# Cosine similarity of rows: loading the last block in thirteen shrinking pieces of x and y in turn, chaining its sums, and storing its results as a column

## The chip, the cores and the metric

The kernel runs on one core of one Trainium2 chip. The time of a run is the time of one execution on the device, in microseconds (us). The profile is one further execution, and its span (first to last instruction) is about 2 us shorter than the time: 1254.4 us of 1256.4 us for the kernel before. Runs of one kernel agree within about 0.8 us here (b_col, one of the experiments: 1.3 us).

Names of engines: DVE is VectorE, ACT is ScalarE, PE is TensorE, SP is SyncE, which issues the DMA transfers. "SPq" in a line is SP's sequencer.

## The reference, cut to what matters

Two float32 inputs, 8192 rows of 8192 columns each; one float32 result per row.

```python
def reference(x, y):                       # 8192 x 8192 each
    x_norm = np.linalg.norm(x, axis=1, keepdims=True)
    y_norm = np.linalg.norm(y, axis=1, keepdims=True)
    return np.sum(x * y, axis=1) / (x_norm.squeeze() * y_norm.squeeze() + 1e-8)
```

Each element is read once: 537 MB in all. The work on a row is three sums: x·y, x·x and y·y.

## The kernel before

The rows form 64 blocks of 128. A block is a tile of x and a tile of y, 128 partitions by 8192 columns, 4 MB each, with two buffers per input. For every block but the last, each tile is loaded by one transfer; DVE sums x·y over the whole tile, and ACT squares and sums x, then y:

```python
nc.vector.tensor_tensor_reduce(out=prod_s, in0=xt, in1=yt, scale=1.0, scalar=0.0,
    op0=mult, op1=add, accum_out=xy_acc[:, t:t + 1])
nc.scalar.activation(out=sq_s, in_=xt, func=Square, accum_out=xx_acc[:, t:t + 1])
nc.scalar.activation(out=sq_s, in_=yt, func=Square, accum_out=yy_acc[:, t:t + 1])
```

The last block (number 63) is loaded as x in two halves, then y in pieces of 2048, 2048, 2048, 1024 and 1024 columns. Its end is what this document is about:

```python
# [cut: DVE squares the first 2048 columns of x, ACT the other 6144]
for k, (a, b) in enumerate(YCH):           # five pieces of y
    nc.scalar.activation(out=sq_s[:, a:b], in_=yt[:, a:b], func=Square, accum_out=yyp[:, k:k + 1])
    nc.vector.tensor_tensor_reduce(out=prod_s[:, a:b], in0=xt[:, a:b], in1=yt[:, a:b],
        scale=1.0, scalar=0.0, op0=mult, op1=add, accum_out=xyp[:, k:k + 1])
# [cut: fold the partial sums; nn = xx*yy; den = sqrt(nn); rcp = 1/den; res = xy*rcp, two columns]
nc.tensor.transpose(out=res_t_ps_last[0:2, :], in_=res[:, tcols], identity=ident)
nc.vector.tensor_copy(out=res_row_last[0:2, :], in_=res_t_ps_last[0:2, :])
nc.sync.dma_start(out=out_v[last - 1:last + 1, :], in_=res_row_last[0:2, :])
```

A result column has one value in each of the 128 partitions. The transpose turns it into a row, so the store writes 512 bytes in one piece for each block.

Of the kernel before, what the change touches and what calls it, by code (L numbers as in the profile page):

```python
# [7 lines left out]


@with_exitstack  # L10
def kernel(
# [6 lines left out]
    nc = tc.nc  # L18
    P = nc.NUM_PARTITIONS

    n_rows, n_cols = x.shape
    assert n_rows % P == 0
    n_tiles = n_rows // P

    fp32 = mybir.dt.float32
    bf16 = mybir.dt.bfloat16

    xv = x.rearrange("(t p) k -> t p k", p=P)
    yv = y.rearrange("(t p) k -> t p k", p=P)

    xpool = ctx.enter_context(tc.tile_pool(name="xpool", bufs=2))
    ypool = ctx.enter_context(tc.tile_pool(name="ypool", bufs=2))
    sqpool = ctx.enter_context(tc.tile_pool(name="sqpool", bufs=1))
    prodpool = ctx.enter_context(tc.tile_pool(name="prodpool", bufs=1))
    accpool = ctx.enter_context(tc.tile_pool(name="accpool", bufs=1))
    finpool = ctx.enter_context(tc.tile_pool(name="finpool", bufs=1))
    psumpool = ctx.enter_context(tc.tile_pool(name="psum", bufs=1, space=bass.MemoryType.PSUM))

    xtiles = [
        xpool.tile([P, n_cols], fp32, tag="x", name=f"xt{t}")  # L40
        for t in range(n_tiles)
    ]
    ytiles = [
        ypool.tile([P, n_cols], fp32, tag="y", name=f"yt{t}")
        for t in range(n_tiles)
    ]

    last = n_tiles - 1

    HALF = n_cols // 2  # L50

    XCH = [(0, HALF), (HALF, n_cols)]
    Q = n_cols // 8
    YCH = [(0, 2 * Q), (2 * Q, 4 * Q), (4 * Q, 6 * Q), (6 * Q, 7 * Q), (7 * Q, n_cols)]

    def issue_dma(t):
        if t == last:
            for a, b in XCH:
                nc.sync.dma_start(out=xtiles[t][:, a:b], in_=xv[t, :, a:b])  # L59
            for a, b in YCH:  # L60
                nc.sync.dma_start(out=ytiles[t][:, a:b], in_=yv[t, :, a:b])  # L61
        else:
            nc.sync.dma_start(out=xtiles[t], in_=xv[t])  # L63
            nc.sync.dma_start(out=ytiles[t], in_=yv[t])  # L64

    issue_dma(0)
    issue_dma(1)

    dummy = finpool.tile([P, 1], fp32, tag="dummy")
    nc.scalar.memzero(dummy)  # L70
    nc.scalar.sqrt(out=dummy, in_=dummy)  # L71

    ident = finpool.tile([P, P], fp32, tag="ident")
    make_identity(nc, ident)

    xx_acc = accpool.tile([P, n_tiles], fp32, tag="xx")
    yy_acc = accpool.tile([P, n_tiles], fp32, tag="yy")
    xy_acc = accpool.tile([P, n_tiles], fp32, tag="xy")

    prod_s = prodpool.tile([P, n_cols], bf16, tag="prod")  # L80
    sq_s = sqpool.tile([P, n_cols], bf16, tag="sq")

    res = finpool.tile([P, n_tiles], fp32, tag="res")
    nn = finpool.tile([P, n_tiles], fp32, tag="nn")
    den = finpool.tile([P, n_tiles], fp32, tag="den")
    rcp = finpool.tile([P, n_tiles], fp32, tag="rcp")
    res_t_ps = psumpool.tile([n_tiles, P], fp32, tag="res_t_ps")
    res_t = finpool.tile([n_tiles, P], fp32, tag="res_t")
    res_t_ps_last = psumpool.tile([2, P], fp32, tag="res_t_ps_last")
    res_row_last = finpool.tile([2, P], fp32, tag="res_row_last")  # L90
    out_v = out.rearrange("(t p) -> t p", p=P)

    def compute_tile(t):
        xt = xtiles[t]
        yt = ytiles[t]
        nc.vector.tensor_tensor_reduce(  # L96
            out=prod_s,
            in0=xt,
            in1=yt,
            scale=1.0,  # L100
            scalar=0.0,
            op0=mybir.AluOpType.mult,
            op1=mybir.AluOpType.add,
            accum_out=xy_acc[:, t:t + 1],
        )
        nc.scalar.activation(  # L106
            out=sq_s,
            in_=xt,
# [28 lines left out]
    for t in range(n_tiles - 1):  # L137
        if t + 2 < n_tiles:
            issue_dma(t + 2)
# [114 lines left out]
```

## Time and profile before

| | |
|---|---|
| time | 1256.36 us (1256.19 to 1256.38, 3 runs) |
| span of the profiled run | 1254.4 us |
| period of a block | 19.4 us (e.g. y of block 61 lands at 1209.5, of block 62 at 1228.9) |
| DVE and ACT work in a block | 8.69 us; 2 x 7.03 + 2 x 0.19 = 14.4 us |
| last load packet, last multiply, end | 1248.9, 1251.66, 1254.4 us |

Lines of the page of the kernel before. In the group lines: line, engine, operation, tiles, shapes, count; then busy us and mean ns of one; then idle time just before them and what ended it.

```profile
span 1254.4 us, 933 instructions
...
q1 hardware_dynamic: 19220, 536.91, 99.5%
...
DMA 76%; DVE 22%; SPq 1%; issue 1%; DVEq 0%; PE 0%; ACT 0%
...
L96 DVE CUSTOM_DVE_ANT_0 prod_s<-xt,yt 128x8192 bf16<-128x8192 f32 x63 | 547.6, 8692 | 687.5 <-DMA yt<-in_y_dram 687.5
...
L112 ACT ACTIVATE sq_s<-yt 128x8192 bf16<-128x8192 f32 x63 | 443.0, 7031 | 164.2 <-DMA yt<-in_y_dram 164.2
...
L186 DVE CUSTOM_DVE_ANT_0 prod_s<-xt,yt 128x2048 bf16<-128x2048 f32 (+1 forms) x5 | 9.2, 1864 | 1.6 <-DMA yt<-in_y_dram 1.5
```

The load queue is busy 99.5% of the time, and DVE sits idle for 687.5 us before its whole-block products, until a load of y lands. So the loads bound the kernel, and only what comes after the last loads, the tail, can be shortened.

The view by stretches of the kernel before, with busy time of each engine, then the granted clock, the DMA share and GB/s:

```profile
...
core 0: us, PE busy (x) PEld busy (x) DVE busy (x) ACT busy (x) POOL busy (x), PEclk, DMA share, GB/s
...
1236.00:1246.00 10.00, 0.00 (x0) 0.00 (x0) 8.59 (x8) 9.38 (x10) 0.00 (x0) 1.00 1.00 413
1246.00:1249.00 3.00, 0.00 (x0) 0.00 (x0) 2.82 (x3) 3.00 (x5) 0.00 (x0) 1.00 0.18 70
1249.00:1252.45 3.45, 0.37 (x1) 0.08 (x1) 2.60 (x9) 1.85 (x7) 0.00 (x0) 1.00 0.00 0
1252.45:1254.40 1.95, 0.00 (x0) 0.00 (x0) 0.00 (x0) 0.00 (x0) 0.00 (x0) 1.00 0.00 1
```

From 1246 us on, most DMA engines have finished and a few lagging ones carry on (share 0.18). In the last 1.95 us no compute engine works: that is the store. The timeline of the same kernel (start us, length us, engine, line, operation) shows the steps between:

```profile
...
1236.10 1.91 ACT L167 ACTIVATE sq_s<-xt 128x2048 bf16<-128x2048 f32 x1
...
1248.17 1.04 ACT L180 ACTIVATE sq_s<-yt 128x1024 bf16<-128x1024 f32 x1
...
1249.21 1.04 ACT L180 ACTIVATE sq_s<-yt 128x1024 bf16<-128x1024 f32 x1
...
1249.55 1.22 DVE L186 CUSTOM_DVE_ANT_0 prod_s<-xt,yt 128x1024 bf16<-128x1024 f32 x1
...
1250.38 0.21 ACT L200 ACTIVATE yy_fold_s<-yyp 128x5 f32<-128x5 f32 x1
...
1250.81 0.16 DVE L204 TENSOR_REDUCE xy_acc<-xyp 128x1 f32<-128x5 f32 x1
...
1251.07 0.20 ACT L212 ACTIVATE den<-nn 128x2 f32<-128x2 f32 x1 [0.39 <-DVE nn L208]
...
1251.50 0.16 DVE L217 TENSOR_TENSOR res<-xy_acc,rcp 128x2 f32<-128x2 f32 x1
...
1251.72 0.37 PE L221 MATMUL res_t_ps_last<-ident,res 128*2 128x128 f32 x1 [31.64 <-DVE res L217]
1252.13 0.28 DVE L222 COPY res_row_last<-res_t_ps_last 2x128 f32<-2x128 f32 x1 [0.46 <-PE res_t_ps_last L221]
1252.43 0.27 SPq L223 DMA_DIRECT2D out_dram<-res_row_last  x1
```

The last product ends at 1249.55 + 1.22 = 1250.77, the last multiply at 1251.50 + 0.16 = 1251.66; the transpose and the copy take until 1252.41; from the issue of the store (1252.43) to the end of the span are 1.97 us. A backlog is work that is ready but has to queue for its engine.

### The profile page before, as it was taken

Reading aid. Unit: us, or ns where it says so; the run is one execution under the profiler, and the core shown is the slowest. Engines: PE = TensorE matmul, PEld = TensorE weight load, DVE = VectorE, ACT = ScalarE, POOL = GpSimd, SP = SyncE. Lnnn points to the kernel's source line nnn. Section 1 sums busy time; section 2 is a strip of 40 time slices with the busy share of each in tenths; the row PEclk is TensorE's granted clock in tenths of the full one; section 3 lists DMA queues with packets and bytes.
Section 4 is the critical chain, followed back from the end, with each engine's and each line's share of the span. In section 5 each row is a group of like instructions: output and inputs, shape, how many; then the busy total and the mean of one; then the engine's idle time right before and its main releaser. Section 6 shows DMA issues by size and latency. Waiting matters only on the chain.

```text
span 1254.4 us, 933 instructions
## 1 busy us (share of the span) xinstructions
PE 0.8 (0%) x2; PEld 0.2 (0%) x2; DVE 561.6 (45%) x147; ACT 915.0 (73%) x276; POOL 0.7 (0%) x6
## 2 busy tenths in 40 slices
PE   0000000000000000000000000000000000000000
PEld 0000000000000000000000000000000000000000
DVE  2354353443534535445354353453544525445356
ACT  5777767776777767776777767776777767776777
POOL 0000000000000000000000000000000000000000
DMA  9999999999999999999999999999999999999997
GB/s 401 435 435 435 429 430 428 435 434 435 429 429 430 434 433 435 429 428 432 434 434 435 428 428 432 435 434 434 428 428 433 435 433 433 427 430 432 435 434 307
DMA packets 19227, 536.97 MB, mean 428 GB/s; under 512 B 2132, under 2 KB 2196, under 8 KB 2452
## 3 DMA queue, kind: packets, MB, share of 16 engines
q1 hardware_dynamic: 19220, 536.91, 99.5%
q14 instruction: 7, 0.06, 0.0%
HBM read 536.87 MB, written 0.03 MB: 428 GB/s over the span
## 4 chain that ended last, share of the span: by engine, by line
DMA 76%; DVE 22%; SPq 1%; issue 1%; DVEq 0%; PE 0%; ACT 0%
DMA yt<-in_y_dram 76%; DVE prod_s L96 21%; SPq L63 1%; DVE prod_s L186 0%; DVEq L96 0%; SPq L64 0%; SPq L61 0%; SPq L59 0%; DVE xy_acc L96 0%; PE res_t_ps_last L221 0%; DVE res_row_last L222 0%; ACT den L212 0%; DVE rcp L216 0%; DVE res L217 0%; DVE xy_acc L204 0%
## 5 line engine op out<-in xcount | busy, mean ns | idle before, releaser
L96 DVE CUSTOM_DVE_ANT_0 prod_s<-xt,yt 128x8192 bf16<-128x8192 f32 x63 | 547.6, 8692 | 687.5 <-DMA yt<-in_y_dram 687.5
L106 ACT ACTIVATE sq_s<-xt 128x8192 bf16<-128x8192 f32 x63 | 442.9, 7031 | 168.5 <-DMA xt<-in_x_dram 168.5
L112 ACT ACTIVATE sq_s<-yt 128x8192 bf16<-128x8192 f32 x63 | 443.0, 7031 | 164.2 <-DMA yt<-in_y_dram 164.2
L112 ACT ACTIVATION_READ_ACCUMULATOR sq_s<-yt 128x1 f32 x63 | 11.8, 188 | 0.0
L106 ACT ACTIVATION_READ_ACCUMULATOR sq_s<-xt 128x1 f32 x63 | 11.8, 187 | 0.0
L186 DVE CUSTOM_DVE_ANT_0 prod_s<-xt,yt 128x2048 bf16<-128x2048 f32 (+1 forms) x5 | 9.2, 1864 | 1.6 <-DMA yt<-in_y_dram 1.5
L180 ACT ACTIVATE sq_s<-yt 128x2048 bf16<-128x2048 f32 (+1 forms) x5 | 7.8, 1551 | 0.0
L96 DVE DVE_READ_ACCUMULATOR2_ANT xy_acc<- 128x1 f32 x63 | 5.2, 83 | 0.0
L173 ACT ACTIVATE sq_s<-xt 128x4096 bf16<-128x4096 f32 x1 | 3.6, 3617 | 0.6 <-DMA xt<-in_x_dram 0.6
L157 DVE CUSTOM_DVE_ANT_0 prod_s<-xt 128x2048 bf16<-128x2048 f32 x1 | 2.3, 2291 | 0.0
L167 ACT ACTIVATE sq_s<-xt 128x2048 bf16<-128x2048 f32 x1 | 1.9, 1911 | 0.0
L70 ACT ACT_TABLE_LOAD x1 | 1.3, 1283 | 0.7 <-PEq L238 0.7
L124 ACT ACTIVATE den<-nn 128x62 f32<-128x62 f32 x1 | 0.3, 257 | 1.8 <-DVE nn L120 1.8
L71 ACT ACT_TABLE_LOAD x1 | 1.3, 1283 | 0.0
L133 PE MATMUL res_t_ps<-ident,res 128*62 128x128 f32 x1 | 0.4, 392 | 1219.7 <-DVE res L129 1219.7
L180 ACT ACTIVATION_READ_ACCUMULATOR sq_s<-yt 128x1 f32 x5 | 0.9, 186 | 0.0
L128 DVE RECIPROCAL rcp<-den 128x62 f32<-128x62 f32 x1 | 0.5, 541 | 0.3 <-ACT den L124 0.3
L134 DVE COPY res_t<-res_t_ps 62x128 f32<-62x128 f32 x1 | 0.3, 282 | 0.6 <-PE res_t_ps L133 0.6
L212 ACT ACTIVATE den<-nn 128x2 f32<-128x2 f32 x1 | 0.2, 204 | 0.4 <-DVE nn L208 0.4
L222 DVE COPY res_row_last<-res_t_ps_last 2x128 f32<-2x128 f32 x1 | 0.3, 278 | 0.5 <-PE res_t_ps_last L221 0.5
L186 DVE DVE_READ_ACCUMULATOR2_ANT xyp<- 128x1 f32 x5 | 0.4, 83 | 0.0
L221 PE MATMUL res_t_ps_last<-ident,res 128*2 128x128 f32 x1 | 0.4, 371 | 31.6 <-DVE res L217 31.6
(23 smaller groups left out, 3.8 us busy)
## 6 DMA issues: line engine op xcount, KB each, us to landing
xt<-in_x_dram SPq DMA_DIRECT2D x63, 4096.0 KB, 20.2
yt<-in_y_dram SPq DMA_DIRECT2D x63, 4096.0 KB, 29.5
xt<-in_x_dram SPq DMA_DIRECT2D x2, 2048.0 KB, 19.9
yt<-in_y_dram SPq DMA_DIRECT2D x3, 1024.0 KB, 24.0
yt<-in_y_dram SPq DMA_DIRECT2D x2, 512.0 KB, 27.1
out_dram<-res_t SPq DMA_DIRECT2D x1, 31.0 KB
out_dram<-res_row_last SPq DMA_DIRECT2D x1, 1.0 KB
```

Of the source, the lines that this page charges most:

```text
L63: nc.sync.dma_start(out=xtiles[t], in_=xv[t])
L70: nc.scalar.memzero(dummy)
L71: nc.scalar.sqrt(out=dummy, in_=dummy)
L96: nc.vector.tensor_tensor_reduce(out=prod_s, in0=xt, in1=yt, scale=1.0, scalar=0.0, op0=mybir.AluOpType.mult, op1=mybir.AluOpType.add, acc ...
L106: nc.scalar.activation(out=sq_s, in_=xt, func=mybir.ActivationFunctionType.Square, accum_out=xx_acc[:, t:t + 1],)
L112: nc.scalar.activation(out=sq_s, in_=yt, func=mybir.ActivationFunctionType.Square, accum_out=yy_acc[:, t:t + 1],)
L128: nc.vector.reciprocal(out=rcp[:, cols], in_=den[:, cols])
L157: nc.vector.tensor_tensor_reduce(out=prod_s[:, 0:SPL], in0=xt[:, 0:SPL], in1=xt[:, 0:SPL], scale=1.0, scalar=0.0, op0=mybir.AluOpType.mult ...
L167: nc.scalar.activation(out=sq_s[:, SPL:HALF], in_=xt[:, SPL:HALF], func=mybir.ActivationFunctionType.Square, accum_out=xxp[:, 1:2],)
L173: nc.scalar.activation(out=sq_s[:, HALF:], in_=xt[:, HALF:], func=mybir.ActivationFunctionType.Square, accum_out=xxp[:, 2:3],)
L180: nc.scalar.activation(out=sq_s[:, a:b], in_=yt[:, a:b], func=mybir.ActivationFunctionType.Square, accum_out=yyp[:, k:k + 1],)
L186: nc.vector.tensor_tensor_reduce(out=prod_s[:, a:b], in0=xt[:, a:b], in1=yt[:, a:b], scale=1.0, scalar=0.0, op0=mybir.AluOpType.mult, op1= ...
```

## The change

The intent was a shorter tail: less work behind the last byte, because the last piece has only 256 columns of y, and a shorter chain, because the PE transpose and the copy go. A fold, in what follows, is a small instruction that adds up partial sums; a chained sum starts from an earlier result instead and needs no fold. The earlier results are finished in two batches (48 and 15 columns) instead of one. The 1e-8 of the reference is now added. The diff, cut to its core:

```diff
+    PIECES = [("x", 3072), ("y", 3072), ("x", 1536), ("y", 1536), ("x", 1536), ("y", 1536),
+              ("x", 768), ("y", 768), ("x", 512), ("y", 512), ("x", 768), ("y", 512),
+              ("y", 256)]
 # loads of the last block
-            for a, b in XCH:
-                nc.sync.dma_start(out=xtiles[t][:, a:b], in_=xv[t, :, a:b])
-            for a, b in YCH:
-                nc.sync.dma_start(out=ytiles[t][:, a:b], in_=yv[t, :, a:b])
+        for which, w in PIECES:
+            a = at[which]
+            at[which] = b = a + w
+            dst, src = (xs, xv) if which == "x" else (ys, yv)
+            nc.sync.dma_start(out=dst[t][:, a:b], in_=src[t, :, a:b])
 # sums of the last block: the first four pieces of x on ACT, the last two on DVE
+        if which == "x":
+            if nx < 4:
+                square(xt[:, a:b], p["xx"][:, nx:nx + 1])
+            else:
+                if nx == 4:
+                    nc.vector.tensor_reduce(out=fold[:, 0:1], in_=p["xx"][:, 0:4], ...)
+                init = fold[:, 0:1] if nx == 4 else p["xx"][:, nx - 1:nx]
+                dot(xt[:, a:b], xt[:, a:b], p["xx"][:, nx:nx + 1], init)
+            nx += 1
+            continue
+        if i == len(PIECES) - 1:
+            nc.vector.tensor_reduce(out=fold[:, 1:2], in_=p["yy"][:, 0:ny], ...)
+        square(yt[:, a:b], p["yy"][:, ny:ny + 1])
+        dot(xt[:, a:b], yt[:, a:b], p["xy"][:, ny:ny + 1], p["xy"][:, ny - 1:ny] if ny else 0.0)
 # [cut: the two square roots on ACT, that of y with the fold as bias; dl = yn*xn + 1e-8; 1/dl]
-    nc.tensor.transpose(out=res_t_ps_last[0:2, :], in_=res[:, tcols], identity=ident)
-    nc.vector.tensor_copy(out=res_row_last[0:2, :], in_=res_t_ps_last[0:2, :])
-    nc.sync.dma_start(out=out_v[last - 1:last + 1, :], in_=res_row_last[0:2, :])
+    nc.vector.tensor_mul(out=rl, in0=p["xy"][:, ny - 1:ny], in1=dl)
+    nc.sync.dma_start(out=ov[last, :].rearrange("(p o) -> p o", o=1), in_=rl)
```

Here `square` is an ACT square with a sum, and `dot` a DVE product with a sum that starts from the value `init`.

More of the change, by code (lines that the diff above doesn't have):

```diff
@@ L7 @@
 from concourse._compat import with_exitstack
+FP32 = mybir.dt.float32
+BF16 = mybir.dt.bfloat16
+ALU = mybir.AluOpType
+ACTF = mybir.ActivationFunctionType
+EPS = 1e-8
 @with_exitstack
@@ L19 @@
     P = nc.NUM_PARTITIONS
-    n_rows, n_cols = x.shape
-    assert n_rows % P == 0
-    n_tiles = n_rows // P
-    fp32 = mybir.dt.float32
-    bf16 = mybir.dt.bfloat16
+    n_rows, K = x.shape
+    nt = n_rows // P
+    last = nt - 1
+    BULK = 48
     xv = x.rearrange("(t p) k -> t p k", p=P)
     yv = y.rearrange("(t p) k -> t p k", p=P)
+    ov = out.rearrange("(t p) -> t p", p=P)
     xpool = ctx.enter_context(tc.tile_pool(name="xpool", bufs=2))
     ypool = ctx.enter_context(tc.tile_pool(name="ypool", bufs=2))
-    sqpool = ctx.enter_context(tc.tile_pool(name="sqpool", bufs=1))
@@ L34 @@
-    prodpool = ctx.enter_context(tc.tile_pool(name="prodpool", bufs=1))
-    accpool = ctx.enter_context(tc.tile_pool(name="accpool", bufs=1))
-    finpool = ctx.enter_context(tc.tile_pool(name="finpool", bufs=1))
-    psumpool = ctx.enter_context(tc.tile_pool(name="psum", bufs=1, space=bass.MemoryType.PSUM))
-    xtiles = [
-        xpool.tile([P, n_cols], fp32, tag="x", name=f"xt{t}")
-        for t in range(n_tiles)
-    ]
-    ytiles = [
-        ypool.tile([P, n_cols], fp32, tag="y", name=f"yt{t}")
-        for t in range(n_tiles)
-    ]
@@ L48 @@
-    last = n_tiles - 1
-    HALF = n_cols // 2
-    XCH = [(0, HALF), (HALF, n_cols)]
-    Q = n_cols // 8
-    YCH = [(0, 2 * Q), (2 * Q, 4 * Q), (4 * Q, 6 * Q), (6 * Q, 7 * Q), (7 * Q, n_cols)]
-    def issue_dma(t):
-        if t == last:
-            for a, b in XCH:
-                nc.sync.dma_start(out=xtiles[t][:, a:b], in_=xv[t, :, a:b])
-            for a, b in YCH:
-                nc.sync.dma_start(out=ytiles[t][:, a:b], in_=yv[t, :, a:b])
-        else:
-            nc.sync.dma_start(out=xtiles[t], in_=xv[t])
-            nc.sync.dma_start(out=ytiles[t], in_=yv[t])
@@ L66, with load @@
-    issue_dma(0)
-    issue_dma(1)
-    dummy = finpool.tile([P, 1], fp32, tag="dummy")
+    small = ctx.enter_context(tc.tile_pool(name="small", bufs=1))
+    psumpool = ctx.enter_context(
+        tc.tile_pool(name="psum", bufs=1, space=bass.MemoryType.PSUM))
+    PIECES = [("x", 3072), ("y", 3072), ("x", 1536), ("y", 1536), ("x", 1536), ("y", 1536),
+              ("x", 768), ("y", 768), ("x", 512), ("y", 512), ("x", 768), ("y", 512),
+              ("y", 256)]
+    xs, ys = {}, {}
+    def load(t):
+        xs[t] = xpool.tile([P, K], FP32, tag="x", name=f"xt{t}")
+        ys[t] = ypool.tile([P, K], FP32, tag="y", name=f"yt{t}")
+        if t < last:
+            nc.sync.dma_start(out=xs[t], in_=xv[t])
+            nc.sync.dma_start(out=ys[t], in_=yv[t])
+            return
+        at = {"x": 0, "y": 0}
+        for which, w in PIECES:
[3 more added lines that the diff above has]
+            nc.sync.dma_start(out=dst[t][:, a:b], in_=src[t, :, a:b])
@@ L70 @@
+    load(0)
+    load(1)
+    xx = small.tile([P, nt], FP32, tag="xx")
+    yy = small.tile([P, nt], FP32, tag="yy")
+    xy = small.tile([P, nt], FP32, tag="xy")
+    den = small.tile([P, 2, nt], FP32, tag="den")
+    res = small.tile([P, nt], FP32, tag="res")
+    ident = small.tile([P, P], FP32, tag="ident")
+    dummy = small.tile([P, 1], FP32, tag="dummy")
+    junk = small.tile([P, K], BF16, tag="junk")
+    prod = small.tile([P, K], BF16, tag="prod")
     nc.scalar.memzero(dummy)
     nc.scalar.sqrt(out=dummy, in_=dummy)
-    ident = finpool.tile([P, P], fp32, tag="ident")
@@ L74 @@
     make_identity(nc, ident)
-    xx_acc = accpool.tile([P, n_tiles], fp32, tag="xx")
-    yy_acc = accpool.tile([P, n_tiles], fp32, tag="yy")
-    xy_acc = accpool.tile([P, n_tiles], fp32, tag="xy")
-    prod_s = prodpool.tile([P, n_cols], bf16, tag="prod")
-    sq_s = sqpool.tile([P, n_cols], bf16, tag="sq")
-    res = finpool.tile([P, n_tiles], fp32, tag="res")
-    nn = finpool.tile([P, n_tiles], fp32, tag="nn")
-    den = finpool.tile([P, n_tiles], fp32, tag="den")
-    rcp = finpool.tile([P, n_tiles], fp32, tag="rcp")
@@ L87 @@
-    res_t_ps = psumpool.tile([n_tiles, P], fp32, tag="res_t_ps")
-    res_t = finpool.tile([n_tiles, P], fp32, tag="res_t")
-    res_t_ps_last = psumpool.tile([2, P], fp32, tag="res_t_ps_last")
-    res_row_last = finpool.tile([2, P], fp32, tag="res_row_last")
-    out_v = out.rearrange("(t p) -> t p", p=P)
-    def compute_tile(t):
-        xt = xtiles[t]
-        yt = ytiles[t]
-        nc.vector.tensor_tensor_reduce(
-            out=prod_s,
-            in0=xt,
-            in1=yt,
-            scale=1.0,
-            scalar=0.0,
-            op0=mybir.AluOpType.mult,
-            op1=mybir.AluOpType.add,
-            accum_out=xy_acc[:, t:t + 1],
-        )
-        nc.scalar.activation(
-            out=sq_s,
-            in_=xt,
-            func=mybir.ActivationFunctionType.Square,
-            accum_out=xx_acc[:, t:t + 1],
-        )
-        nc.scalar.activation(
-            out=sq_s,
-            in_=yt,
-            func=mybir.ActivationFunctionType.Square,
-            accum_out=yy_acc[:, t:t + 1],
-        )
@@ L119, in chain @@
-    def chain(cols, ps, sb, orows):
-        nc.vector.tensor_tensor(
-            out=nn[:, cols], in0=xx_acc[:, cols], in1=yy_acc[:, cols],
-            op=mybir.AluOpType.mult,
-        )
-        nc.scalar.activation(
-            out=den[:, cols], in_=nn[:, cols],
-            func=mybir.ActivationFunctionType.Sqrt,
-        )
-        nc.vector.reciprocal(out=rcp[:, cols], in_=den[:, cols])
-        nc.vector.tensor_tensor(
-            out=res[:, cols], in0=xy_acc[:, cols], in1=rcp[:, cols],
-            op=mybir.AluOpType.mult,
-        )
-        nc.tensor.transpose(out=ps, in_=res[:, cols], identity=ident)
-        nc.vector.tensor_copy(out=sb, in_=ps)
-        nc.sync.dma_start(out=out_v[orows, :], in_=sb)
@@ L137 @@
-    for t in range(n_tiles - 1):
-        if t + 2 < n_tiles:
-            issue_dma(t + 2)
-        compute_tile(t)
-        if t == n_tiles - 3:
-            e = slice(0, last - 1)
-            chain(e, res_t_ps[e, :], res_t[e, :], e)
-    lcol = slice(last, last + 1)
-    tcols = slice(last - 1, last + 1)
-    xt = xtiles[last]
-    yt = ytiles[last]
-    SPL = 2048
-    xxp = accpool.tile([P, 3], fp32, tag="xxp")
-    nych = len(YCH)
-    yyp = accpool.tile([P, nych], fp32, tag="yyp")
-    xyp = accpool.tile([P, nych], fp32, tag="xyp")
@@ L154 @@
-    xx_fold_s = accpool.tile([P, 3], fp32, tag="xxfolds")
-    yy_fold_s = accpool.tile([P, nych], fp32, tag="yyfolds")
-    nc.vector.tensor_tensor_reduce(
-        out=prod_s[:, 0:SPL],
-        in0=xt[:, 0:SPL],
-        in1=xt[:, 0:SPL],
-        scale=1.0,
-        scalar=0.0,
-        op0=mybir.AluOpType.mult,
-        op1=mybir.AluOpType.add,
-        accum_out=xxp[:, 0:1],
-    )
-    nc.scalar.activation(
-        out=sq_s[:, SPL:HALF],
-        in_=xt[:, SPL:HALF],
-        func=mybir.ActivationFunctionType.Square,
-        accum_out=xxp[:, 1:2],
-    )
@@ L173 @@
-    nc.scalar.activation(
-        out=sq_s[:, HALF:],
-        in_=xt[:, HALF:],
-        func=mybir.ActivationFunctionType.Square,
-        accum_out=xxp[:, 2:3],
-    )
-    for k, (a, b) in enumerate(YCH):
-        nc.scalar.activation(
-            out=sq_s[:, a:b],
-            in_=yt[:, a:b],
-            func=mybir.ActivationFunctionType.Square,
-            accum_out=yyp[:, k:k + 1],
-        )
-        nc.vector.tensor_tensor_reduce(
-            out=prod_s[:, a:b],
-            in0=xt[:, a:b],
-            in1=yt[:, a:b],
-            scale=1.0,
-            scalar=0.0,
-            op0=mybir.AluOpType.mult,
-            op1=mybir.AluOpType.add,
-            accum_out=xyp[:, k:k + 1],
-        )
@@ L196 @@
-    nc.scalar.activation(
-        out=xx_fold_s, in_=xxp, func=mybir.ActivationFunctionType.Copy,
-        accum_out=xx_acc[:, lcol],
-    )
-    nc.scalar.activation(
-        out=yy_fold_s, in_=yyp, func=mybir.ActivationFunctionType.Copy,
-        accum_out=yy_acc[:, lcol],
-    )
-    nc.vector.tensor_reduce(
-        out=xy_acc[:, lcol], in_=xyp, axis=mybir.AxisListType.X,
-        op=mybir.AluOpType.add,
-    )
-    nc.vector.tensor_tensor(
-        out=nn[:, tcols], in0=xx_acc[:, tcols], in1=yy_acc[:, tcols],
-        op=mybir.AluOpType.mult,
-    )
@@ L212 @@
-    nc.scalar.activation(
-        out=den[:, tcols], in_=nn[:, tcols],
-        func=mybir.ActivationFunctionType.Sqrt,
-    )
-    nc.vector.reciprocal(out=rcp[:, tcols], in_=den[:, tcols])
-    nc.vector.tensor_tensor(
-        out=res[:, tcols], in0=xy_acc[:, tcols], in1=rcp[:, tcols],
-        op=mybir.AluOpType.mult,
-    )
-    nc.tensor.transpose(out=res_t_ps_last[0:2, :], in_=res[:, tcols], identity=ident)
-    nc.vector.tensor_copy(out=res_row_last[0:2, :], in_=res_t_ps_last[0:2, :])
@@ L223, with square, dot, finish @@
-    nc.sync.dma_start(out=out_v[last - 1:last + 1, :], in_=res_row_last[0:2, :])
+    def square(src, acc):
+        nc.scalar.activation(
+            out=junk[:, 0:src.shape[-1]], in_=src, func=ACTF.Square, accum_out=acc)
+    def dot(a, b, acc, init=0.0):
+        nc.vector.tensor_tensor_reduce(
+            out=prod[:, 0:a.shape[-1]], in0=a, in1=b, scale=1.0, scalar=init,
+            op0=ALU.mult, op1=ALU.add, accum_out=acc)
+    def finish(a, b):
+        n = b - a
+        c = slice(a, b)
+        nc.scalar.activation(out=den[:, 0, c], in_=xx[:, c], func=ACTF.Sqrt)
+        nc.scalar.activation(out=den[:, 1, c], in_=yy[:, c], func=ACTF.Sqrt)
+        nc.vector.tensor_mul(out=den[:, 0, c], in0=den[:, 0, c], in1=den[:, 1, c])
+        nc.vector.tensor_scalar_add(out=den[:, 0, c], in0=den[:, 0, c], scalar1=EPS)
+        nc.vector.reciprocal(out=den[:, 1, c], in_=den[:, 0, c])
+        nc.vector.tensor_mul(out=res[:, c], in0=xy[:, c], in1=den[:, 1, c])
+        ps = psumpool.tile([n, P], FP32, tag=f"ps{a}", name=f"ps{a}")
+        row = small.tile([n, P], FP32, tag=f"row{a}", name=f"row{a}")
+        nc.tensor.transpose(out=ps, in_=res[:, c], identity=ident)
+        nc.vector.tensor_copy(out=row, in_=ps)
+        nc.sync.dma_start(out=ov[c, :], in_=row)
@@ new lines @@
+    for t in range(last):
+        if t + 2 < nt:
+            load(t + 2)
+        xt, yt = xs.pop(t), ys.pop(t)
+        dot(xt, yt, xy[:, t:t + 1])
+        square(xt, xx[:, t:t + 1])
+        square(yt, yy[:, t:t + 1])
+        if t == BULK:
+            finish(0, BULK)
+    xt, yt = xs.pop(last), ys.pop(last)
+    p = {n: small.tile([P, 8], FP32, tag=f"p{n}", name=f"p{n}") for n in ("xx", "yy", "xy")}
+    fold = small.tile([P, 2], FP32, tag="fold")
+    nx = ny = 0
+    at = {"x": 0, "y": 0}
@@ new lines @@
+    for i, (which, w) in enumerate(PIECES):
+        a = at[which]
+        at[which] = b = a + w
+        if which == "x":
[3 more added lines that the diff above has]
+                if nx == 4:
+                    nc.vector.tensor_reduce(
+                        out=fold[:, 0:1], in_=p["xx"][:, 0:4], axis=mybir.AxisListType.X,
+                        op=ALU.add)
+                init = fold[:, 0:1] if nx == 4 else p["xx"][:, nx - 1:nx]
[3 more added lines that the diff above has]
+        if i == len(PIECES) - 1:
+            nc.vector.tensor_reduce(
+                out=fold[:, 1:2], in_=p["yy"][:, 0:ny], axis=mybir.AxisListType.X, op=ALU.add)
+        square(yt[:, a:b], p["yy"][:, ny:ny + 1])
+        dot(xt[:, a:b], yt[:, a:b], p["xy"][:, ny:ny + 1],
+            p["xy"][:, ny - 1:ny] if ny else 0.0)
+        ny += 1
+        if i == 1:
+            finish(BULK, last)
@@ new lines @@
+    xn = small.tile([P, 1], FP32, tag="xn")
+    yn = small.tile([P, 1], FP32, tag="yn")
+    dl = small.tile([P, 1], FP32, tag="dl")
+    rl = small.tile([P, 1], FP32, tag="rl")
+    nc.scalar.activation(out=xn, in_=p["xx"][:, nx - 1:nx], func=ACTF.Sqrt)
+    nc.scalar.activation(
+        out=yn, in_=p["yy"][:, ny - 1:ny], func=ACTF.Sqrt, bias=fold[:, 1:2])
+    nc.vector.tensor_scalar(
+        out=dl, in0=yn, scalar1=xn, scalar2=EPS, op0=ALU.mult, op1=ALU.add)
+    nc.vector.reciprocal(out=dl, in_=dl)
```

## The prediction

> **What bounds the kernel now.** The loads. The page's DMA section shows one hardware queue busy for 99.5% of 16 engines' span, at 428 GB/s. The chain of waits is 76% loads of y. In the groups, DVE sits idle 687.5 us before the products and ACT 168.5 and 164.2 us before the squares, for loads. The period is 19.4 us a block, against 8.69 us of DVE and 14.4 us of ACT. Loads for block t+2 are issued when block t's product ends, about 10 us before the queue would run dry, so the change does not touch the steady blocks; the two earlier `finish` calls run in idle DVE and ACT time.
>
> **The tail.** In 0.1 us stretches, the DMA share falls from 1.0 at 1246.1 us, and a few lagging engines, at last one, carry on to 1248.9; the span ends at 1254.4: 5.5 us of tail. By the timeline, the last two products are backlogged (no idle before them) and end at 1250.77; fold, product, sqrt, reciprocal, multiply, transpose and copy take until 1252.41; the store takes the last 2.0 us (issue 0.27).
>
> **What changes, costed.** DVE products take 2292 ns at 2048 columns and 1221 at 1024, which agrees with the (N+151)/0.96 ns that the Trainium skill gives for a float32 tensor_tensor add ("VectorE: DVE Perf Modes", "The TRN2 errata"). Estimates from that: 768 columns 0.96, 512 0.69, 256 0.42 us. From ACT squares (1892 and 1039 ns): 256 columns 0.40 us, plus 0.19 for the accumulator read.
> - Removed behind the last product: PE transpose 0.39 and PSUM copy 0.28, 0.7 us; the fold of xy, 0.16; ACT's Copy folds.
> - Added: two squared x pieces on DVE (512 and 768), two folds, load issues (0.42 us each on SP, hidden behind a queue over 10 us deep).
> - DVE stays backlogged: a lagging engine delivers 256 columns in 0.33 us (2.7 us for the last 2048 columns before). With the last byte at 0, DVE does y768 until -2.3, then fold, x512, y512, x768, y512, fold, y256 without a gap, ending at about +1.9 (before: +1.9 too). ACT has both square roots by +1.7. Then dl, reciprocal, multiply (0.17 each): about +2.6, against +3.5 before. Shrinking the last piece buys little of itself; the gain is the shorter chain behind it.
> - Store: 128 runs of 4 bytes instead of 2 rows of 512. The skill, "DMA: Bandwidth & Descriptors", "Specifications", says that below 512 B the engines read, modify and write; no trace here shows its cost. I allow 0.2 us. Load rows of 1 to 3 KB: 0.1 us.
>
> **On the critical path:** -0.9 + 0.3 = -0.6 us. The 1e-8 is fused and free.
>
> **Predicted:** 1255.7 us, 8 in 10 between 1254.5 and 1257.0; faster by over 2% 0.5%, within 2% 98.5%, slower 1%.
>
> **What would show it.** Same 19.4 us period; last load bytes at about 1248.9; no DVE idle before the last five products; last multiply about 2.6 us after the last byte; no PE at the end; about 2.2 us from that multiply to the end.
>
> **What would make it wrong.** The 4-byte store taking a microsecond or more longer; short load rows slowing the lagging engine; the lag itself shifting; ACT late with y's squares so that the last fold stalls DVE; or a gap between the loads, as pieces wait for earlier ones to land before they are issued.

## The result, and the profile after

The changed kernel takes 1264.51 us (1264.31 to 1264.93, 4 runs); the kernel before, in the same and earlier rounds, 1256.34 us. The ratio is 1.0066 (95% interval 1.0051 to 1.008). A ratio here is the mean time of one kernel's runs over that of the other's of the same rounds, so it isn't quite the ratio of the medians quoted. The change lost 8.2 us where a gain of 0.6 was predicted.

Lines of the page of the changed kernel:

```profile
span 1262.5 us, 974 instructions
...
q1 hardware_dynamic: 20254, 536.91, 99.0%
...
L85 DVE CUSTOM_DVE_ANT_0 prod<-xt,yt 128x8192 bf16<-128x8192 f32 x64 | 551.0, 8609 | 688.0 <-DMA yt<-in_y_dram 688.0
```

The steady part is unchanged: DVE's idle time before the products is 688.0 us (687.5 before), and y of block 62 lands at 1229.1 us (1228.9 before). The loss is in the tail. The view by stretches of the changed kernel, same columns:

```profile
...
1236.00:1246.00 10.00, 0.39 (x1) 0.10 (x1) 9.34 (x12) 9.87 (x12) 0.00 (x0) 1.00 1.02 407
1246.00:1249.00 3.00, 0.00 (x0) 0.00 (x0) 1.54 (x4) 2.94 (x5) 0.00 (x0) 1.00 0.35 125
1249.00:1254.20 5.20, 0.00 (x0) 0.00 (x0) 4.50 (x15) 3.69 (x12) 0.00 (x0) 1.00 0.00 0
1255.00:1255.25 0.25, 0.00 (x0) 0.00 (x0) 0.00 (x0) 0.00 (x0) 0.00 (x0) 1.00 0.31 2
1255.25:1262.50 7.25, 0.00 (x0) 0.00 (x0) 0.00 (x0) 0.00 (x0) 0.00 (x0) 1.00 0.00 0
```

The last load data still move until just before 1249 us. Compute now goes on until 1254.2 instead of 1251.7. Then the DMA engines' records of the store lie within a quarter of a microsecond (1255.00 to 1255.25), and for 7.25 us after that nothing moves and nothing computes. The timeline of the changed kernel, some of its lines:

```profile
...
1229.12 7.03 ACT L81 ACTIVATE junk<-yt 128x8192 bf16<-128x8192 f32 x1 [2.30 <-DMA yt<-in_y_dram]
...
1236.28 2.76 ACT L81 ACTIVATE junk<-xt 128x3072 bf16<-128x3072 f32 x1
...
1245.27 1.48 ACT L81 ACTIVATE junk<-xt 128x1536 bf16<-128x1536 f32 x1
...
1246.88 1.48 ACT L81 ACTIVATE junk<-yt 128x1536 bf16<-128x1536 f32 x1
...
1249.45 0.16 DVE L129 TENSOR_REDUCE fold<-pxx 128x1 f32<-128x4 f32 x1 [1.88 <-ACT junk L81]
...
1252.41 0.40 ACT L81 ACTIVATE junk<-yt 128x256 bf16<-128x256 f32 x1
...
1253.10 0.48 DVE L85 CUSTOM_DVE_ANT_0 prod<-xt,yt,pxy 128x256 bf16<-128x256 f32 x1
1253.22 0.29 ACT L151 ACTIVATE yn<-pyy,fold 128x1 f32<-128x1 f32 x1 [0.33 <-DVE fold L137]
...
1254.00 0.16 DVE L156 TENSOR_TENSOR rl<-pxy,dl 128x1 f32<-128x1 f32 x1
1254.19 0.35 SPq L157 DMA_DIRECT2D out_dram<-rl  x1
```

ACT is still squaring y of block 62 until 1236.15, starts the last block only then, and ends its last square at 1252.81. DVE is idle for 1.88 us before 1249.45, where its fold of x's sums waits for ACT. The last multiply ends at 1254.16.

The kernel before started its last block from the same backlog (ACT at 1236.10), and its last square ended at 1250.25. So the backlog alone is not what the change added. By the two timelines, ACT has more to do in the last block: 11 squares over 15104 columns take 14.80 us, where 7 squares over 14336 columns took 13.28. And it now pauses between squares: eight times it starts the next one only 0.12 to 0.13 us after the last has ended (1245.27 + 1.48 = 1246.75, the next at 1246.88), where before the squares of y follow without a pause (1248.17 + 1.04 = 1249.21). In the trace each square of the changed kernel waits for the semaphore that ACT's own reads of the sums raise; the squares of y before wait for their loads alone. The code has a likely reason: all squares now write their unused products to the same columns, `junk[:, 0:w]`, while before each piece had columns of its own, `sq_s[:, a:b]`. No run gives the pieces separate columns, so what these pauses cost at the end, and their reason, are not shown.

What SP waited for at the end, in the view of waits of the DMA queue (us in total, times, longest), in the kernel before:

```profile
...
SPq L249 <- DMA out_dram<-res_row_last: 0.6, 1, 0.6
```

And in the changed kernel, the same view:

```profile
...
SPq L183 <- DMA out_dram<-rl: 6.8, 1, 6.8
```

The landing of the store is waited for 6.8 us instead of 0.6.

The difference of the spans, 8.1 us, is made up as follows, all from the two timelines:

| step | before | after | difference |
|---|---|---|---|
| last multiply ends (us) | 1251.66 | 1254.16 | +2.50 |
| from there to the issue of the store | 0.77 | 0.03 | -0.74 |
| from the issue to the end of the span | 1.97 | 8.31 | +6.34 |
| sum | | | +8.10 |

So there are two losses to explain, the store and late arithmetic, and one gain that came as planned.

### The profile page after: what moved, and what is told of

The parts are those of the page before. It is cut to its first block, busy times and chain, and to the rows that moved or that the text cites. A ratio compares the mean times of both kernels' runs of the same rounds, so it can differ in the third digit from the quotient of the medians.

```text
span 1262.5 us, 974 instructions
## 1 busy us (share of the span) xinstructions
PE 0.8 (0%) x2; PEld 0.2 (0%) x2; DVE 562.8 (45%) x159; ACT 917.3 (73%) x284; POOL 0.7 (0%) x6
## 4 chain that ended last, share of the span: by engine, by line
DMA 74%; DVE 22%; issue 2%; SPq 1%; ACT 0%; DVEq 0%
DMA yt<-in_y_dram 74%; DVE prod L85 21%; SPq L53 1%; ACT junk L81 0%; DVEq L85 0%; DVE xy L85 0%; SPq L54 0%; DVE dl L153 0%; DVE pxx L85 0%; DVE pxy L85 0%; DVE dl L155 0%; DVE fold L129 0%; DVE rl L156 0%; DVE fold L137 0%; ACT den L94 0%
## 5 line engine op out<-in xcount | busy, mean ns | idle before, releaser
L85 DVE CUSTOM_DVE_ANT_0 prod<-xt,yt 128x8192 bf16<-128x8192 f32 x64 | 551.0, 8609 | 688.0 <-DMA yt<-in_y_dram 688.0
L81 ACT ACTIVATE junk<-xt 128x8192 bf16<-128x8192 f32 (+2 forms) x67 | 449.4, 6708 | 170.7 <-DMA xt<-in_x_dram 170.6
L81 ACT ACTIVATE junk<-yt 128x8192 bf16<-128x8192 f32 (+3 forms) x70 | 451.1, 6444 | 163.8 <-DMA yt<-in_y_dram 163.7
L81 ACT ACTIVATION_READ_ACCUMULATOR junk<-yt 128x1 f32 x70 | 13.1, 186 | 0.0
L81 ACT ACTIVATION_READ_ACCUMULATOR junk<-xt 128x1 f32 x67 | 12.5, 186 | 0.0
L85 DVE CUSTOM_DVE_ANT_0 prod<-xt,yt,pxy 128x1536 bf16<-128x1536 f32 (+3 forms) x6 | 6.6, 1104 | 0.1
L85 DVE DVE_READ_ACCUMULATOR2_ANT xy<- 128x1 f32 x63 | 5.2, 82 | 0.0
```

The source lines that it names most:

```text
L81: nc.scalar.activation(out=junk[:, 0:src.shape[-1]], in_=src, func=ACTF.Square, accum_out=acc)
L85: nc.vector.tensor_tensor_reduce(out=prod[:, 0:a.shape[-1]], in0=a, in1=b, scale=1.0, scalar=init, op0=ALU.mult, op1=ALU.add, accum_out=acc)
```

## The experiments

The theory after the comparison: the column store costs about 6 us because of how its 4-byte runs (a run of bytes is what a transfer writes in one piece) are written, and the arithmetic is late because DVE and ACT, not the loads, end last. The rivals: the loads became slower in short rows or in the new order; the price of the store belongs to the DMA engines or to any column; the last loads end the chain and the engines only follow them.

Kernels ran with their own runs of the kernel before, whose median stayed between 1256.29 and 1256.36 us. Kernels that gave a wrong result on purpose ran once and are read by their profile alone. They are written as edits of the changed kernel unless said otherwise.

### The store put back to a row: a_row

```diff
-    nc.sync.dma_start(out=ov[last, :].rearrange("(p o) -> p o", o=1), in_=rl)
+    nc.tensor.transpose(out=psl, in_=rl, identity=ident)
+    nc.vector.tensor_copy(out=rowl, in_=psl)
+    nc.sync.dma_start(out=ov[last:last + 1, :], in_=rowl)
```

> The changed kernel, with only the last store put back to a transpose, a copy and one row of 512 bytes. Theory: of the 8.2 us that the change lost, about 6.3 are the column store (from its issue to the end of the span 8.35 us, before 2.0), and about 1.7 to 2.6 are late arithmetic (last multiply ends at 1254.2 us, before 1251.7). So it expects the store tail back at 2.0 us, the last multiply where the change has it (1254.2), and the time at 1264.5 - 6.3 + 0.75 for transpose and copy = 1259.0 us, still 2 to 3 us slower than before. Rival (the loads in short rows, or the new order of loads, made the whole kernel slower and the store only waits for it): 1262 us or more.

Measured: 1258.65 us (1258.62 to 1258.73), ratio 1.0019 (1.0003 to 1.0036). The last multiply ends at 1254.04, the store is issued at 1254.81 and the span ends at 1256.8, 2.0 us later. A line of its timeline:

```profile
...
1253.88 0.16 DVE L156 TENSOR_TENSOR rl<-pxy,dl 128x1 f32<-128x1 f32 x1
```

SP's wait for the store, in the view of waits:

```profile
...
SPq L187 <- DMA out_dram<-rowl: 0.7, 1, 0.7
```

So the column store cost 1264.51 - 1258.65 = 5.9 us net of the transpose and copy that it saves, and the arithmetic alone leaves the kernel 2.3 us slower than before. The rival, that the loads had become slower (1262 us or more), falls.

### The column store alone, in the kernel before: b_col

```diff
-    nc.tensor.transpose(...); nc.vector.tensor_copy(...); nc.sync.dma_start(..., in_=res_row_last[0:2, :])
+    nc.sync.dma_start(out=out_v[last - 1:last + 1, :].rearrange("t p -> p t"), in_=res[:, tcols])
```

> The kernel before, with only its last two result columns stored as a column: 256 runs of 4 bytes to two neighbouring stretches of 512 bytes, without transpose and copy. Theory S (runs to one stretch of 512 bytes go one after the other): two stretches, either side by side, about 8.3 us from issue to end as with one, or in line, about 14.7. Theory E (each DMA engine does its runs one after the other, about 0.8 us each from 6.4 us for 8): 16 runs an engine, about 14.7 us. Theory F (a fixed price for a column, whatever its size): 8.3 us. Removed transpose and copy give back about 0.75 us. Time 1256.3 - 0.75 + 6.3 = 1262 us, or 1268 us.

Measured: 1264.66 us (1263.95 to 1265.27), ratio 1.0067 (1.0052 to 1.0082). From issue (1252.26) to end of span (1263.5) are 11.2 us, between the two values that the theories gave. The store alone makes the kernel before as slow as the whole change did; that the two totals agree is chance, since here 256 runs cost more and the arithmetic is not late. 256 runs in two neighbouring stretches cost more than 128 in one, but not twice as much.

### Where the runs lie: a_far, a_s64, a_sp16

The same transfer, with the runs 256 bytes apart, 64 bytes apart, and (32 runs) 16 bytes apart.

```diff
-    nc.sync.dma_start(out=ov[last, :].rearrange("(p o) -> p o", o=1), in_=rl)
+    a_far:  out=out.rearrange("(p t) -> p t", p=P)[:, last:last + 1], in_=rl
+    a_s64:  out=out[0:2048].rearrange("(p o) -> p o", o=16)[:, 15:16], in_=rl
+    a_sp16: out=ov[last, :].rearrange("(p o) -> p o", o=4)[:, 3:4], in_=rl[0:32, :]
```

> Wrong result on purpose: the changed kernel's 128 runs of 4 bytes are written 256 bytes apart over the whole output, instead of side by side in one stretch of 512 bytes; the same number of runs on each DMA engine. Theory S: the runs no longer meet in one place, tail from issue to end about 2 to 2.5 us. Theory E and theory F: 8.3 us as before.

> Wrong result on purpose: the changed kernel's 128 runs of 4 bytes over 16 engines, 64 bytes apart (at 256 bytes they were fast, at 4 bytes slow). If the runs collide within a 64-byte unit or less, the store is fast, issue to end about 2.3 us. If the unit is larger, two to four runs share one and some of the 6 us remains: 2.5 to 5 us.

> Wrong result on purpose: 32 values, 16 bytes apart, over one stretch of 512 bytes (4 in each 64 bytes). If the price depends on the number of runs in 64 bytes: as 64 bytes apart, nothing more than a row. If it depends on the number of runs in a larger stretch (256 or 512 bytes): as the 32 runs side by side.

SP's wait for the store in a_far, from the view of waits:

```profile
...
SPq L183 <- DMA out_dram<-rl: 0.9, 1, 0.9
```

The same view of a_s64:

```profile
...
SPq L183 <- DMA out_dram<-rl: 0.9, 1, 0.9
```

The same view of a_sp16:

```profile
...
SPq L183 <- DMA out_dram<-rl: 0.8, 1, 0.8
```

All three are as quick as a row, give or take 0.2 us (0.6 to 0.7 us in the six kernels that store one row of 512 bytes). The number of runs, the size of a run and the number of runs on each DMA engine are the same in the first two as in the changed kernel, where SP waited 6.8 us. So it isn't the 4-byte run that is dear; it is 4-byte runs packed side by side. These are single runs, but the gap of 6 us is far above the spread. Theories E and F fall here.

### How many runs, and from how many DMA engines: a_17, a_32, a_61, a_64, c_127

Only the first n values are stored, or, in c_127, all of them by two transfers of 1 and 127 values:

```diff
+    a_17, a_32, a_61, a_64:  out=ov[last, 0:n].rearrange("(p o) -> p o", o=1), in_=rl[0:n, :]
+    c_127:  the same for rl[127:128, :] and then for rl[0:127, :]
```

> Wrong result on purpose: only the first 17 values of the column are stored. By the Trainium skill, DMA: Bandwidth & Descriptors, Why a DMA increments its semaphore by 16, such a transfer goes to a single DMA engine. Theory S: 17 runs in one place, about 17 x 0.05 = 0.85 us more than a row, tail about 2.9 us. Theory E: 17 runs on one engine, about 17 x 0.8 = 13.6 us more, tail about 15 us. Theory F: 8.3 us.

> The changed kernel, correct, with the same column stored by two transfers, one of 1 value and one of 127, which by the Trainium skill (DMA: Bandwidth & Descriptors, Why a DMA increments its semaphore by 16) each go to a single DMA engine. Theory S2 (formed after the far runs and the 17 runs were both fast: the price is paid when several DMA engines write short runs into the same place): 127 runs from one engine cost about what 17 do, plus one more issue: last multiply to end of span 2.6 to 3.5 us, time about 1258.5 us. Rival S1 (each short run into the same stretch costs about 0.05 us, whichever engine writes it): about 6 us more, about 1264.5 us.

> Wrong result on purpose: only the first 64 values of the column are stored (16 engines, 4 runs each, all in one half of a stretch of 512 bytes). So far 17 runs cost next to nothing over a row, 127 or 128 runs about 6.3 us more, and 256 in two stretches about 9 us more. Theory S1 (each run into the stretch beyond a first few costs about 0.055 us): 64 runs cost 2.5 to 3.2 us more, issue to end about 5 us. Rival T (a threshold: the price falls due at once when a stretch is filled, or with the eighth run of an engine): tail about 2.3 us.

> Wrong result on purpose: only the first 32 values of the column are stored (16 engines, 2 runs each). Measured so far, from the end of the issue to the landing: a row 0.8 us; 17 runs 1.0; 64 runs 6.1; 128 runs 7.0. Theory B (the first 16 or so runs into a place are free, then each costs about 0.11 us until another place is reached): 32 runs cost 1.8 us more than a row. Theory C (runs into the same 64 bytes chain, 16 of them, whichever stretch): as 64 runs, 5 to 6 us more. Theory N (price only for more than 32): nothing more.

> Wrong result on purpose: only the first 61 values of the column are stored; 61 is prime, so by the same section of the Trainium skill the transfer goes to one DMA engine, where 64 values go to 16. If the place decides, not the number of engines: 61 runs from one engine cost within 1.5 us of what 64 from 16 cost (landing 6.1 us after the issue). If short runs of several engines have to meet, one engine with 61 is as fast as with 17, about 1 to 1.5 us (but 127 from one engine were slow).

| kernel | runs, side by side | DMA engines | issue, us | SP's wait for the landing, us |
|---|---|---|---|---|
| a_row | 1 of 512 bytes | 1 | 0.26 | 0.7 |
| a_17 | 17 | 1 | 0.26 | 0.8 |
| a_32 | 32 | 16 | 0.35 | 2.8 |
| a_61 | 61 | 1 | 0.26 | 7.3 |
| a_64 | 64 | 16 | 0.55 | 5.9 |
| c_127 | 127 (after 1) | 1 | 0.24 | 7.7 |
| changed kernel | 128 | 16 | 0.35 | 6.8 |
| b_col | 256, two stretches | 16 | 0.42 | 9.7 |

Three of these as the view of waits has them. First a_17:

```profile
...
SPq L183 <- DMA out_dram<-rl: 0.8, 1, 0.8
```

The same view of a_61:

```profile
...
SPq L183 <- DMA out_dram<-rl: 7.3, 1, 7.3
```

The same view of c_127, whose two stores are waited for together:

```profile
...
SPq L185 <- DMA out_dram<-rl: 8.0, 2, 7.7
```

After a_far and a_17 were both quick, the theory S2 was that several DMA engines have to meet in one place. c_127 refuted it: one engine with 127 runs is as slow as 16 engines with 8 each, 1265.57 us (1265.14 to 1265.83). a_61 (one engine, 7.3 us) against a_64 (16 engines, 5.9 us) says the same. That the engines are one or sixteen is the rule of the Trainium skill, "DMA: Bandwidth & Descriptors", "Why a DMA increments its semaphore by 16 and not by 1"; the trace agrees as far as it shows it, for the store's semaphore was updated 16 times in the changed kernel, between 1257.5 and 1261.6 us, and twice in a_17. The other kernels of the table follow: 16 updates in a_32, a_64 and b_col, two in a_row, a_61 and for the 127 runs of c_127.

A constant price for each run falls too: 17 runs cost 0.1 us more than a row, 32 cost 2.1, 64 cost 5.2 and 128 cost 6.1. Theories T (2.3 us for 64 runs), C (32 as dear as 64) and N (32 free) each missed. Theory B put 1.8 on 32 runs, where 2.1 were measured, but it had been fitted to 17 and 64 runs, and its 5 us for 61 runs fall short of the 6.6 over a row. It is a candidate, not a finding. Sixteen runs within 64 bytes are not enough to make a store dear (a_17 has them), and 32 runs spread over 512 bytes are not either (a_sp16). What is shown is what a kernel needs: 17 packed 4-byte runs were cheap, 32 and more were dear, and a gap between them (16 bytes from start to start at 32 runs, 64 at 128 runs) or one run of 512 bytes avoids it. Where the price begins is not shown for either number of engines: the 17 came from one engine, which was next tried with 61, and with 16 engines fewer than 32 were not tried. The mechanism stays open.

### Fewer pieces, and no fold in the middle: r_coarse, r_nofold, r_cnf

These three start from a_row (1258.65 us), so that the store is out of the way. r_coarse has 7 pieces instead of 13; r_nofold no longer chains x's sums on DVE to ACT's; r_cnf does both.

```diff
 r_coarse:
+    PIECES = [("x", 3072), ("y", 3072), ("x", 3072), ("y", 3072), ("x", 2048), ("y", 1024), ("y", 1024)]
 r_nofold:
-                if nx == 4: nc.vector.tensor_reduce(out=fold[:, 0:1], in_=p["xx"][:, 0:4], ...)
-                dot(xt[:, a:b], xt[:, a:b], p["xx"][:, nx:nx + 1], init)
+                dot(xt[:, a:b], xt[:, a:b], p["xx"][:, nx:nx + 1])
 # after the last piece
+    nc.vector.tensor_reduce(out=fold[:, 0:1], in_=p["xx"][:, 0:nx], ...)
+    nc.scalar.activation(out=xn, in_=fold[:, 0:1], func=ACTF.Sqrt)
```

> The kernel of the row store (1258.65 us), with the last block in 7 pieces instead of 13 (x 3072, y 3072, x 3072, y 3072, x 2048 squared on DVE, y 1024, y 1024). Theory P (ScalarE and VectorE, not the loads, end last; each further piece costs ScalarE about 0.37 us beyond its columns): ScalarE ends its squares at about 1250.6 instead of 1252.8, last multiply at about 1252 instead of 1254.0, time about 1256.5 us. Rival L (the last loads end the chain; a larger last piece leaves more work behind the last byte): the last piece has 1024 columns instead of 256, so 0.8 us later, about 1259.5 us.

> The kernel of the row store (1258.65 us), 13 pieces, with the two late x sums of VectorE not chained by initial values to a fold of ScalarE's x sums: all six x sums are folded at the end. Theory Q (two engines end together: the fold makes VectorE wait 1.9 us for ScalarE's backlog, and without that wait VectorE would stand where ScalarE stands): the wait of 1.9 us at the fold goes, but ScalarE's squares end where they did, about 1252.5, so the last multiply moves from 1254.0 to about 1253.6 only, time about 1258.2 us. Rival (the fold's wait is the whole of the delay): 1256.8 us.

> Both at once: 7 pieces and x sums folded at the end. 7 pieces alone moved nothing (1258.52 us against 1258.65), since ScalarE gained and VectorE then waited 2.0 us at the fold. Theory Q: with both, ScalarE ends its squares at about 1250.2 and VectorE its products at about 1251.7, last multiply about 1252.4 instead of 1254.0, time about 1256.9 us. Rival L (the last loads decide): no better than either alone, 1258.2 us.

| kernel | time, us | last multiply ends, us | DVE's wait at a fold, us |
|---|---|---|---|
| a_row | 1258.65 (1258.62 to 1258.73) | 1254.04 | 1.9 |
| r_coarse | 1258.52 (1258.34 to 1258.74) | 1254.06 | 2.0 |
| r_nofold | 1258.00 (1257.74 to 1258.49) | 1253.16 | 1.0 |
| r_cnf | 1257.28 (1257.24 to 1257.54) | 1252.81 | none |

The fold in the view of waits of DVE, in r_coarse:

```profile
...
DVE fold L127 <- ACT junk L80: 2.0, 1, 2.0
```

And in r_nofold:

```profile
...
DVE fold L132 <- ACT junk L81: 1.0, 1, 1.0
```

The expectation for r_coarse missed: theory P had put it at 1256.5. ACT gained, but DVE's fold still waited for ACT's second piece of x, and the product behind it waited in turn. With the fold moved, only part of the wait came back in another place (the fold of y, 1.0 us). Both edits together bring 1.4 us, more than the 0.1 and the 0.65 of each. So neither the number of pieces nor the fold alone makes the arithmetic late; both engines are short of time, and freeing one leaves the other. The expected 1256.9 of r_cnf was 0.4 too low. The place of an instruction in its engine's queue counts too: in a_row the product of x with 512 columns stood behind the fold until 1249.52, and in r_nofold, without that fold, it started at 1247.38. All three kernels keep the shared scratch columns and the small `finish` in the last block, so they leave these two untested.

### The block before the last in halves: r_62

From a_row; the last block and its 13 pieces are untouched.

```diff
+        if t == last - 1:                      # loads: x half, y half, x half, y half
+            for a in (0, K // 2):
+                h = slice(a, a + K // 2)
+                nc.sync.dma_start(out=xs[t][:, h], in_=xv[t, :, h])
+                nc.sync.dma_start(out=ys[t][:, h], in_=yv[t, :, h])
 # and in the loop: one dot and two squares on each half, the two sums of x and of y added on DVE
```

> The kernel of the row store (1258.65 us) with the block before the last loaded and worked on in halves of x and y in turn; the last block keeps its 13 pieces. Theory P: the two engines start the last block 3 to 4 us earlier (in the changed kernel they finish the block before at 1236.1 and 1237.9, because its y came whole at 1229), catch up with the loads, and idle before the last pieces; last multiply about 1251.0, time about 1255.5 us. Rival L (the loads end the chain): no change, about 1258.6 us.

Measured: 1256.34 us (1256.24 to 1256.46), ratio to the kernel before 1.0 (0.9985 to 1.0015): 2.3 us better than a_row, by an edit outside the last block. Lines of the timeline of r_62:

```profile
...
1233.90 2.75 ACT L87 ACTIVATE junk<-xt 128x3072 bf16<-128x3072 f32 x1
...
1247.06 0.16 DVE L147 TENSOR_REDUCE fold<-pxx 128x1 f32<-128x4 f32 x1
...
1250.01 0.40 ACT L87 ACTIVATE junk<-yt 128x256 bf16<-128x256 f32 x1
...
1251.61 0.16 DVE L174 TENSOR_TENSOR rl<-pxy,dl 128x1 f32<-128x1 f32 x1
```

ACT starts the last block at 1233.90 instead of 1236.28, the fold of x finds its sums ready, and the last multiply ends at 1251.77. Against a_row itself, ACT's start (1236.14), the fold (1249.33) and the end of the last multiply (1254.04) all come 2.2 to 2.3 us earlier: what ACT gains at the start arrives whole at the end. The rival that the loads end the chain of a_row falls. One side effect: the `finish` of the 15 columns, unchanged in the source, now runs on DVE at 1234.0 instead of 1241.2. In a_row DVE idled 1.9 us at the fold after it, so that shift alone can't explain the gain. With the backlog gone, the tail of the 13 pieces is close to the one that the prediction had drawn for the change: last multiply at 1248.9 + 2.6 = 1251.5.

### Two tries to beat both kernels: best, best2

Both have the halves of r_62 and x's sums folded at the end. best has 8 pieces (x 4096, y 4096, x 2048, y 2048, x 1024 squared on DVE, x 1024, y 1024, y 1024), and turns the results with DVE's 32 by 32 transpose to store 4 rows of 128 bytes. best2 keeps a_row's store and has

```diff
+    PIECES = [("x", 3328), ("x", 2048), ("y", 2304), ("y", 2048), ("x", 768), ("y", 1280),
+              ("x", 512), ("y", 1024), ("x", 1024), ("y", 512), ("y", 512), ("x", 512), ("y", 512)]
 # DVE squares the two pieces of x with 512 columns, ACT the other four
```

> Meant to beat both kernels: the block before the last in halves, the last block in 8 pieces (x 4096, y 4096, x 2048, y 2048, x 1024 squared on VectorE, x 1024, y 1024, y 1024), x sums folded at the end, and the last results turned by VectorE's 32 by 32 transpose and stored as 4 rows of 128 bytes. Theory Q, estimate: last multiply at about 1251.6 us, transpose 0.2, store tail about 2.0 us; span about 1253.9, time about 1255.7 us against 1256.36 before. If the 4 rows in one stretch of 512 bytes collide like the single values, some 0.2 us more.

> A second try to beat both: the block before the last in halves, row store, x sums folded at the end, and the last block in 13 pieces whose late ones are short and of y, with most of x squared on ScalarE before. Estimate from the durations measured so far: last multiply at about 1251.4 us against 1251.77 in the kernel with halves alone (1256.34 us), time about 1256.0 us; a gain of more than 1 us on the kernel before is not expected, since the last byte lands at 1249.3 and the chain and store behind it take 5 us at the least.

best missed: 1256.70 us (1256.47 to 1257.19), ratio 1.0003 (0.999 to 1.0017). Its last multiply came at 1251.81, 0.2 us after the estimate, and the saving of the transpose was lost at its store: the issue took 0.63 us instead of 0.26, and SP waited 1.0 us for the landing instead of 0.6. The end of the timeline of best:

```profile
...
1251.85 0.21 DVE L173 STREAM_TRANSPOSE rt<-rl 128x32 f32<-128x32 f32 x1
1252.09 0.63 SPq L174 DMA_DIRECT2D out_dram<-rt  x1
```

best2 takes 1255.80 us (1255.76 to 1255.83, 5 runs) against 1256.33 us (1256.16 to 1256.69, 9 runs) of the kernel before: all its runs lie below all of those. Its ratio is 0.9995 (0.9982 to 1.0009), so by the interval it isn't told apart from 1. Its last multiply ends at 1251.30, 0.36 us before that of the kernel before. It is the fastest of all kernels here, by 0.5 us.

## Why the prediction was wrong, point by point

- **"Loads bound the kernel", "the change does not touch the steady blocks": right.** 688.0 us of idle time before the products against 687.5, and the same last load packet, near 1248.8.
- **"Store ... I allow 0.2 us": wrong, and the largest error.** The store took 8.31 us from issue to end, not 2.2. The term was 6.3 us in place of 0.2. Part of the blame is the reasoning behind it: the prediction took a run below 512 bytes as the thing that costs, as the skill's table has it, and gave it a small allowance. The runs showed that 128 runs of 4 bytes, 64 or 256 bytes apart, cost next to nothing (and 32 of them 16 bytes apart), and that 128 side by side cost 6 us. It was named among what could make the prediction wrong, but the sum set only 0.2 us aside for it.
- **"With the last byte at 0, DVE does y768 until -2.3, then fold, ... without a gap": wrong, worth 2.7 us.** This step counted back from the landings as if ACT's sums were there whenever DVE needed them. With the last byte at 1248.9, the y768 product should have ended at 1246.6 and ended at 1247.57; then the fold waited 1.88 us for ACT, which reached the end of the fourth piece of x only at 1249.32. "No DVE idle before the last five products" was falsified by that line, and the last multiply came at 1254.16 against 1251.5. ACT's time was never added up in the prediction: its square of block 62's y lasts until 1236.15, while pieces of the last block land, and from 1236 on it worked 9.87 of 10 us and 2.94 of the next 3. The kernel before was nearly as busy (9.38 and 3.00) and started from the same backlog, so by the timelines the prediction missed the sum of two things: a backlog that was there already, and 1.5 us more of squares, with pauses between them, on top of it. r_62 takes the backlog away and gets 1251.77; r_nofold takes DVE's wait for the fold of x away and gains 0.9 us of the 2.7. How the rest divides between the squares, the pauses and the order of the pieces is not shown.
- **"The two earlier `finish` calls run in idle DVE and ACT time": half right.** The second ran on DVE from 1241.3 to 1242.9 us, in the midst of the backlog. What that cost was not tried by itself; as DVE idled 1.88 us at the fold afterwards, it can have cost little here.
- **"0.7 us" for the removed transpose and copy: right.** 0.74 us from the two timelines.
- **"Shrinking the last piece buys little of itself": nothing speaks against it.** With the store out of the way (a_row), the thirteen pieces were 2.3 us slower than the kernel before, and with the backlog out of the way too (r_62), equal to it; r_coarse, with a last piece of 1024 columns, took as long as a_row with 256. No run changed the last piece alone.
- **"A gap between the loads": did not come.** The DMA share from 1236 to 1246 us is 1.02.

In sum: -0.6 predicted, +8.1 in the spans. The store's term was 6.1 us too small. The arithmetic's was 2.7 us too small: -0.9 predicted up to the issue of the store, with the saved transpose and copy in it, and +2.50 - 0.74 = +1.76 measured. The 0.1 allowed for short load rows was not needed.

## What to carry to other kernels

Cost a tail forward from when each engine comes free, not backward from when data lands: an engine that still works on the block before does not see small pieces as small, and chunking the last-but-one block can be worth more than chunking the last. Treat a store of one value per partition into adjacent addresses as a cost to measure before a transpose is removed for it, even if it is a few hundred bytes; turn the values into a row, or leave gaps between them. When two engines are both short of time, an edit that frees one may show little (0.1 and 0.65 us here); try the pair (1.4 us).

## What the Trainium skill lacked or had wrong

- "DMA: Bandwidth & Descriptors", "Specifications" gives 512 bytes as the least transfer for full rate, with read-modify-write below. It lacks that short writes cost by how they are packed: SP waited 0.9 us for 128 runs of 4 bytes 64 or 256 bytes apart, as for a row of 512 bytes (0.7), and 6.8 us for the same runs side by side. It has no figure for the number of packed runs either: 17 (from one engine) cost 0.8 us, 32 (from 16) cost 2.8, 64 (from 16) cost 5.9.
- The same page, "Anatomy of one DMA", says of transfers issued by GpSimd that the wait for the confirmed write is most of their fixed cost, about 2 us. The store here was issued by SP, on a queue of the other kind ("hardware_dynamic"), for which the section has no such split. The trace fits the same reading, with the store's records over by 1255.25 us and its last semaphore update at 1261.6, but that wait was 6 us for 512 bytes; that it is the confirmed write that takes so long is not shown.
- "VectorE: DVE Perf Modes", "The TRN2 errata" gives (N+151)/0.96 ns for a float32 add of two tensors. The product with a sum that starts from 0 agrees (2292 ns at 2048 columns, 0.69 us at 512 in r_nofold). The product whose sum starts from an earlier result takes about 0.06 us more (0.75 us at 512, 1.02 against 0.96 at 768), which no page that was read has.
